# A retention head's keys: transposed by DMA in two planes of 16-bit halves, with the position factor on the values

## The chip, the cores and the metric

The kernel runs on one core of a Trainium2 chip. Its time is the device time of the whole program in microseconds, as the median of several runs. A core has a matrix engine (TensorE, PE in the profile), three engines for elementwise work (VectorE, DVE; ScalarE, ACT; GpSimd, POOL) and SyncE (SP), which here does nothing but issue DMAs, one after the other in one queue.

## The reference

One layer of a decoder in float32: 2048 tokens of width 1024, with 16 learned meta tokens ahead of them. The projection `w_in` gives eight groups of 512 columns. Four of them feed a gated short convolution, four a retention with 4 heads of width 128, computed in chunks of 128 tokens.

```python
hn = rms_norm(h, norm_g)                       # h: 16 meta tokens, then 2048 tokens
cx, cb, cc, cg, q, k, v, rg = split(hn @ w_in, 8)
conv_out = cb * causal_conv3(cc * cx) * silu(cg)
q, k = rotary(q, pos) * 128**-0.5, rotary(k, pos)        # 4 heads of width 128
# per head, with decay g per token, chunks n of 128 tokens, i and j positions in a chunk:
inner = ((q @ k.T) * g**(i - j) * (i >= j)) @ v
upd   = (k * g**(127 - j)).T @ v                         # sums over the chunk's tokens
state_next = g**128 * state + upd
cross = (q * g**(i + 1)) @ state
ret   = head_group_norm(inner + cross) * silu(rg)        # norm over the head's 128 columns
out   = rms_norm(h + concat(conv_out, ret) @ w_out, final_g)
```

The product `upd` sums over tokens, so it needs k and v with the tokens on the partitions. The projections come out of TensorE the other way, with the head's 128 columns on the partitions. Both k and v have to be transposed, chunk by chunk. The score product needs k untransposed.

## The kernel before

**Rounds and units.** The 2048 tokens are worked in two rounds of 1024, each as two halves `j` = 0 and 1 of 512 tokens (4 chunks). A round runs eight units: 0 to 3 are the heads, 4 to 7 the convolution groups. Round 0 takes them as 4, 0, 1, 2, 3, 5, 6, 7, round 1 as 0 to 7. The output projection with `w_out` follows.

**Quads.** A unit consists of two quads of projections; those of a head make K and V, and then Q and RG (the gate). A quad multiplies two blocks of weights by two of tokens with seven products instead of eight (Strassen's scheme in Winograd's form). A product is four steps in the contraction with three matmuls each (line L232), because every float32 operand is split in a high and a low part: low weight by high data, high by low, high by high. The products add up in PSUM banks named `pj`. Product 5 adds onto the bank that holds product 3, and ScalarE must have copied product 3 out before (`tc`, L239). The weights come by DMA (`ra`, L487, eight buffers), GpSimd forms their block sums, ScalarE casts the high part (`wh`, L110), VectorE subtracts for the low part (`wl`, L122); both lie in rings of three buffers, so the cast of one product's weights waits until TensorE has finished the product three before it.

**A head.** VectorE applies the rotary table to K and Q (L648 to L651). V goes through `part` and `cross`: ScalarE copies the float32 values apart into a plane of low and one of high 16-bit halves (`pl`, L667), SP issues a DMA that transposes each 128x128 block of both planes (`tr`, L660), and later `join` on ScalarE puts the halves together (`v`, L745) and multiplies each chunk by `rc2`, the squared row norms' factor (L748). After the second quad, for each half j: TensorE transposes the four chunks of K into PSUM (L768), ScalarE copies them out and multiplies by the position factor `kd_col`, which is g**-(j + 1) in column h (`kd`, L770), and TensorE makes four state updates (`up`, L777), which VectorE adds onto the decayed states (L780). Then follow the scores (L790), their mask on VectorE (`pm`, L792) with a factor `past_col` per row, the two products of the output (L800, L801) and the norm (L806 to L817). The normalised output is turned back during the next unit by the same means (`turn`: `apart`, L823, and `cross`; `finish`: L829 and L831).

**What sets the order.** The framework that builds the program schedules each engine's instructions by a model of time; hints of the form `issue_after` hold a step behind another instruction. The second quad calls a list of `steps`, one after each copied bank (after products 0, 2 and 3). For a head of the kernel before they are `split_late`, which takes V's half 0 apart, and the join of V's half 0; the join of half 1 follows the quad. Tiles named `kd`, `pm` and `t1` share a pool of two buffers (`brief`); `pl`, `tr`, `v`, `kv`, `qg` and others share a pool of sixteen (`gen`).

In round 0 each head also multiplies the meta tokens with its weights (L445) and makes its first state of them (L475).

Of the kernel before, what the change touches and what calls it, by code (L numbers as in the profile page):

```python
# [8 lines left out]
F32 = mybir.dt.float32  # L9
# [4 lines left out]
ALU = mybir.AluOpType  # L14

P = 128
# [4 lines left out]
NG = 4  # L21
EPS = 1e-6
HB = 512
NR = 2
# [23 lines left out]
def retention_constants():  # L48

    import numpy as np  # L50

    half = P // 2
    freqs = (1.0 / (10000.0 ** (np.arange(half) / half))).astype(np.float32)
    pos = np.arange(NMETA + SEQ, dtype=np.float32)
    ang = (freqs[:, None] * pos[None, :]).astype(np.float64)
    cos, sin = np.cos(ang), np.sin(ang)
    rot = np.stack([np.concatenate([cos, cos], 0), np.concatenate([sin, -sin], 0)], 1)

    lg = np.log(np.float32(1.0) - np.float32(2.0) ** (-5.0 - np.arange(NG, dtype=np.float32)))
    lg = lg.astype(np.float32).astype(np.float64)  # L60
    i = np.arange(P, dtype=np.float64)
    causal = (i[None, :] >= i[:, None]).astype(np.float64)
    past = np.stack([np.exp(-(P + i + 1) * g) for g in lg], 1)
    kd = np.stack([np.exp(-(i + 1) * g) for g in lg], 1)
    signed = np.concatenate([-sin[:, :NMETA], sin[:, :NMETA]], 0)
    rot_m = np.stack([np.concatenate([cos[:, :NMETA]] * 2, 0), signed], 0).transpose(2, 0, 1)
    rot_m = rot_m[:, :, None, :] * kd[P - NMETA :, None, :, None]
    row = np.stack([np.exp((P + i + 1) * g) * P**-0.5 for g in lg], 1)
    cols = np.concatenate([kd, EPS / (row * row), past], 1)
    chunk_decay = [float(np.exp(P * g)) for g in lg]  # L70
    return {
        "rot": rot.astype(np.float32),
        "rot_m": rot_m.reshape(NMETA, 2, NG, P).transpose(2, 0, 1, 3).astype(np.float32),
        "causal": causal.astype(np.float32),
        "cols": cols.astype(np.float32),
    }, chunk_decay
# [3 lines left out]
def hybrid_trunk(ctx: ExitStack, tc: tile.TileContext, t, out: bass.AP, chunk_decay):  # L80
# [4 lines left out]

    nc = tc.nc
    x = t["x"]

    const = ctx.enter_context(tc.tile_pool(name="const", bufs=1))
    small = ctx.enter_context(tc.tile_pool(name="small", bufs=2))  # L90
# [33 lines left out]
    def load_raw(loads):  # L124
        tiles = []
        for load in loads:
            a = raw()
            load(a)
            tiles.append(a)
        return tiles  # L130
# [213 lines left out]
    ones_r = const.tile([P, 1], F32R, name="ones_r")  # L344
    neg_half = const.tile([P, CH], F32, name="neg_half")
    meta_s = const.tile([P, KT, NMETA], F32, name="meta_s")
    cols = const.tile([P, 3 * NG], F32, name="cols")
    conv_w = const.tile([P, NG, 3], F32, name="conv_w")
    ret_g = const.tile([P, NG], F32, name="ret_g")
    causal = const.tile([P, P], F32, name="causal")  # L350
    conv_carry = [const.tile([P, 2], F32, name=f"carry{g}") for g in range(NG)]
    state = [const.tile([P, P], F32, name=f"state{h}") for h in range(NG)]
    kd_col, eps_col, past_col = (cols[:, NG * i : NG * (i + 1)] for i in range(3))

    def raw():
        return sb.tile([P, HB], F32, name="ra", tag="ra", bufs=RAW)
# [9 lines left out]
    def spread_factors(ss, rr, rr2, two_part):  # L366


        add(nc.vector, ss[:, 0, :], ss[:, 0, :], ss[:, 1, :])
        rc = small.tile([P, CH], F32, name="rc", tag="rc")  # L370
        v = rsqrt_mean(rc, ss[:, 0, :])
        spread(rc, P, rr, rr2, two_part)
        rc2 = small.tile([P, CH], F32, name="rc2", tag="rc2", bufs=2 * NR)
        nc.vector.tensor_tensor(out=rc2, in0=rc, in1=rc, op=ALU.mult)
        ev = small.tile([P, NG, CH], F32, name="ev", tag="ev", bufs=2 * NR)
        nc.vector.tensor_tensor(
            out=ev,
            in0=eps_col.rearrange("p (h c) -> p h c", c=1).broadcast_to([P, NG, CH]),
            in1=v.rearrange("p (h c) -> p h c", h=1).broadcast_to([P, NG, CH]),
            op=ALU.mult,  # L380
        )
        return rc2, ev

    def row_tile(name, pair):
        return sb.tile([P, BLK], F32, name=name, tag=f"rr{pair}", bufs=2)
# [298 lines left out]
    def head(h, r, m, rot_t, f, turning, blocks, ahead, sums, first=(), between=((), idle, idle)):  # L684
# [37 lines left out]
        def take(i, j, pp, c):  # L722
# [9 lines left out]
            else:  # L732
# [3 lines left out]
                nc.vector.tensor_tensor(out=d, in0=pp, in1=f[0][:, j * HB : (j + 1) * HB], op=ALU.mult)  # L736
                sg[j] = d

        def split_late():
            for j in late:  # L740
                v[j] = part(v[j])

        def join(j):
            a = gen("v")[:, :HB]
            nc.scalar.copy(out=halves(a), in_=planes(v[j]))  # L745
            for c in range(CH):
                cs = slice(c * P, (c + 1) * P)
                nc.scalar.mul(a[:, cs], a[:, cs], f[2][j][0][:, c : c + 1])  # L748
            v[j] = a

        quad(stationary(load_raw(w_loads(2 * h + 1))), m, take, (split_late, lambda: join(0)))
        catch_up(1)
        with tc.issue_after(copied[0].ins):
            join(1)
        between[2]()
        with tc.issue_after(queried[0].ins):
            next(sums, None)
# [5 lines left out]
        states = [state[h]]  # L763
        vt = []
        for j in range(2):
            tp = ps_misc()
            for c in range(CH):
                nc.tensor.transpose(tp[:, c * P : (c + 1) * P], k[j][:, c * P : (c + 1) * P], ident)  # L768
            kd = brief("kd")
            nc.scalar.mul(kd, tp, kd_col[:, h : h + 1])  # L770
            vj = v[j]
            vt.append(vj)
            last = r == NR - 1 and j == 1
            up = ps_misc()
            for c in range(CH - last):
                cs = slice(c * P, (c + 1) * P)
                nc.tensor.matmul(up[:, cs], kd[:, cs], vj[:, cs], start=True, stop=True)  # L777
            for c in range(CH - last):
                nxt = sb.tile([P, P], F32, name="state", tag="state", bufs=2 * CH)
                nc.vector.scalar_tensor_tensor(  # L780
                    out=nxt, in0=states[-1], scalar=chunk_decay[h], in1=up[:, c * P : (c + 1) * P],
                    op0=ALU.mult, op1=ALU.add,
                )
                states.append(nxt)

        for j in range(2):
            sc = ps_misc()
            for c in range(CH):
                cs = slice(c * P, (c + 1) * P)
                nc.tensor.matmul(sc[:, cs], k[j][:, cs], q[j][:, cs], start=True, stop=True)  # L790
            pm = brief("pm")
            nc.vector.scalar_tensor_tensor(  # L792
                out=pm.rearrange("p (c i) -> p c i", c=CH), in0=sc.rearrange("p (c i) -> p c i", c=CH),
                scalar=past_col[:, h : h + 1],
                in1=causal.rearrange("p (c i) -> p c i", c=1).broadcast_to([P, CH, P]), op0=ALU.mult, op1=ALU.mult,
            )
            o = ps_misc()
            for c in range(CH):
                cs = slice(c * P, (c + 1) * P)
                nc.tensor.matmul(o[:, cs], pm[:, cs], vt[j][:, cs], start=True, stop=False)  # L800
                nc.tensor.matmul(o[:, cs], q[j][:, cs], states[j * CH + c], start=False, stop=True)  # L801

            st = small.tile([P, CH, 6], F32, name="st", tag="st")
            mv = small.tile([P, CH, 2], F32, name="mv", tag="mv")
            for c in range(CH):
                nc.vector.bn_stats(out=st[:, c, :], in_=o[:, c * P : (c + 1) * P])  # L806
            for c in range(CH):
                nc.vector.bn_aggr(out=mv[:, c, :], in_=st[:, c, :])
            rs = small.tile([P, CH, 1], F32, name="rs", tag="rs")
            ev = f[2][j][1]  # L810
            add(nc.vector, rs, mv[:, :, 1:2], ev[:, h, :].rearrange("p (c a) -> p c a", a=1))
            rp = small.tile([P, CH, 1], F32, name="rp", tag="rp")
            nc.gpsimd.tensor_tensor(out=rp, in0=rs, in1=neg_half.rearrange("p (c a) -> p c a", a=1), op=ALU.pow)  # L813
            y = pm
            for c in range(CH):
                cs = slice(c * P, (c + 1) * P)
                nc.vector.tensor_scalar(  # L817
                    out=y[:, cs], in0=o[:, cs], scalar1=mv[:, c, 0:1], scalar2=rp[:, c, :],
                    op0=ALU.subtract, op1=ALU.mult,
                )  # L820

            def turn(j=j, y=y, apart=turning[0][:, j * HB : (j + 1) * HB], across=turning[1][:, j * HB : (j + 1) * HB]):
                nc.scalar.copy(out=planes(apart), in_=halves(y))  # L823
                cross(across, apart)

                nc.scalar.activation(sg[j], sg[j], AF.Silu)

                def finish():
                    nc.scalar.copy(out=halves(apart), in_=planes(across))  # L829
                    nc.vector.scalar_tensor_tensor(  # L830
                        out=sg[j], in0=apart, scalar=ret_g[:, h : h + 1], in1=sg[j], op0=ALU.mult, op1=ALU.mult  # L831
                    )
                    store_mixed(r, j, KH + h, sg[j])

                waiting[1].append(finish)

            waiting[0].append(turn)
# [249 lines left out]
```

## Time and profile before

| what | value |
|---|---|
| median of 3 runs (lowest to highest) | 876.3 us (876.18 to 877.04) |
| span of the profiled execution, first to last instruction | 874.9 us |
| PE busy | 863.1 us (99%), clock 0.997 on average |
| PE weight loads (beside the matmuls) | 711.8 us (81%) |
| DVE busy | 717.1 us (82%) |
| ACT busy | 474.8 us (54%) |
| POOL busy | 391.2 us (45%) |
| DMA | 143 GB/s on average |

The runs' times are those of executions without a profile; the profiled execution has its span only, and 874.9 stands 1.4 us below the median, which takes in what lies around the span. A matmul's end in the profile is modelled, so matmuls that follow each other overlap in the rows, and the step from start to start (12 matmuls of a product in 2.73 us) says more than a duration.

### The profile page before, as it was taken

The page shows a single profiled execution, that of the slowest core. Times are in us where ns is not written, and L with a number is a line of the kernel's source. Part 1 is how long each engine was busy: PE and PEld are TensorE (multiplying, and loading weights), DVE is VectorE, ACT ScalarE, POOL GpSimd, SP SyncE. Part 2 cuts the span into 40 slices and gives each one's busy share as a digit, 9 for nine tenths or more (in the row PEclk, how much of TensorE's full clock was granted, in tenths as well). Part 3 has the DMA queues.
Part 4 walks back from the last instruction along what each step waited for, and adds up shares of the span by engine and source line. Part 5 has one row for each costly group of instructions (what it writes and reads, how often), then busy time and mean ns, then how long its engine had stood idle before and what let it go on. Part 6 is the DMA issues. An engine that isn't in the chain of part 4 may idle for free.

```text
span 874.9 us, 12767 instructions
## 1 busy us (share of the span) xinstructions
PE 863.1 (99%) x4280; PEld 711.8 (81%) x4280; DVE 717.1 (82%) x1190; ACT 474.8 (54%) x883; POOL 391.2 (45%) x286
## 2 busy tenths in 40 slices
PE   8999999999999999999999999999999999999996
PEld 5878788878888778888888888888888888788885
DVE  6889898989887887989889898988767799656664
ACT  8675547374644654846464646444333465545553
POOL 0662332333235555352232333354646545678763
PEclk9999999999999999999999999999999999999998
DMA  9723235353556633854243444646222594455432
GB/s 336 220 81 81 63 75 143 109 145 97 129 185 181 190 112 97 292 166 121 61 120 133 108 158 86 214 100 211 64 73 67 172 339 132 162 159 188 154 129 76
DMA packets 110321, 125.32 MB, mean 143 GB/s; under 512 B 41456, under 2 KB 58672, under 8 KB 110256
## 3 DMA queue, kind: packets, MB, share of 16 engines
q1 hardware_dynamic: 109680, 124.11, 46.9%
q8 instruction: 34, 0.56, 0.3%
q10 hardware_dynamic: 576, 0.40, 0.1%
q14 instruction: 31, 0.25, 0.1%
HBM read 90.92 MB, written 25.17 MB: 133 GB/s over the span
## 4 chain that ended last, share of the span: by engine, by line
PE 91%; DVE 5%; issue 1%; ACT 1%; DMA 1%; POOL 0%; ACTq 0%; POOLq 0%; DVEq 0%
PE pj L232 72%; PE pj L289 10%; PE ms L800 2%; PE ms L801 2%; PE ms L790 2%; PE ms L777 1%; PE ms L445 1%; DVE wl L122 1%; PE ms L768 1%; DMA ra<-in_w_in 1%; DVE ml L122 1%; DVE c L523 0%; DVE ml L114 0%; DVE rot L648 0%; DVE yo L870 0%
## 5 line engine op out<-in xcount | busy, mean ns | idle before, releaser
L232 PE MATMUL pj<-mh,wl 128*128 128x512 f32 x1008 | 397.8, 395 | 1.5 <-ACT tc L239 1.2
L232 PE MATMUL pj<-mh,wh 128*128 128x512 f32 x1008 | 393.2, 390 | 0.0
L232 PE MATMUL pj<-ml,wh 128*128 128x512 f32 x1008 | 392.5, 389 | 0.0
L110 ACT CAST wh<-ra 128x512 fp32r<-128x512 f32 x216 | 133.9, 620 | 272.5 <-PE pj L232 226.0
L122 DVE TENSOR_TENSOR wl<-ra,wh 128x512 fp32r<-128x512 f32 x216 | 188.6, 874 | 45.6 <-ACT wh L110 45.1
L232 PEld LDWEIGHTS pj<-mh,wl 128*128 128x128 f32 x1008 | 189.3, 188 | 42.7 <-issue 2.7
L232 PEld LDWEIGHTS pj<-mh,wh 128*128 128x128 f32 x1008 | 189.2, 188 | 40.1
L232 PEld LDWEIGHTS pj<-ml,wh 128*128 128x128 f32 x1008 | 189.4, 188 | 37.8
L119 POOL TENSOR_TENSOR sa<-ra 128x512 f32<-128x512 f32 x36 | 53.0, 1473 | 99.7 <-DMA ra<-in_w_in 50.9
L122 POOL TENSOR_TENSOR ra<-sa,ra 128x512 f32<-128x512 f32 x36 | 51.8, 1438 | 80.2 <-DVE wl L122 79.0
L122 POOL TENSOR_TENSOR ra<-ra 128x512 f32<-128x512 f32 x36 | 58.0, 1611 | 59.4 <-PE ms L445 47.5
L149 POOL TENSOR_TENSOR ra<-ra 128x512 f32<-128x512 f32 x36 | 61.0, 1694 | 39.5 <-issue 26.7
L239 ACT COPY tc<-pj 128x512 f32<-128x512 f32 x108 | 62.6, 580 | 0.0
L289 PE MATMUL pj<-mh,mh 128*128 128x512 f32 x128 | 51.0, 400 | 1.8 <-ACT mh L967 1.1
L289 PE MATMUL pj<-mh,ml 128*128 128x512 f32 x128 | 50.0, 390 | 0.2 <-DVE ml L122 0.2
L289 PE MATMUL pj<-ml,mh 128*128 128x512 f32 x128 | 48.1, 392 | 0.0
L813 POOL TENSOR_TENSOR rp<-rs,neg_half 128x4 f32<-128x4 f32 x16 | 17.8, 1112 | 54.8 <-DVE rs L119 54.7
L870 DVE TENSOR_TENSOR yo<-pj,yo 128x512 f32<-128x512 f32 (+1 forms) x33 | 22.0, 673 | 22.6 <-PE pj L232 15.0
L585 POOL TENSOR_TENSOR c<-c,rr 128x512 f32<-128x512 f32 x14 | 26.4, 1884 | 29.8 <-DVE c L626 18.1
L110 ACT CAST wh<-sa 128x512 fp32r<-128x512 f32 x36 | 22.2, 617 | 22.9 <-PE pj L232 22.9
L876 POOL TENSOR_TENSOR z<-yo,final_g 128x512 f32<-128x512 f32 x16 | 26.0, 1627 | 18.9 <-DVE yo L870 18.9
L817 DVE TENSOR_SCALAR pm<-ms,mv,rp 128x128 f32<-128x128 f32 x64 | 21.9, 404 | 12.4 <-POOL rp L813 12.3
(152 smaller groups left out, 1209.2 us busy)
## 6 DMA issues: line engine op xcount, KB each, us to landing
ra<-in_w_in SPq DMA_DIRECT2D x126, 256.0 KB, 2.8
x<-in_xT SPq DMA_DIRECT2D x48, 256.0 KB, 4.8
w<-in_w_out SPq DMA_DIRECT2D x32, 256.0 KB, 5.0
ra<-mixed SPq DMA_DIRECT2D x32, 256.0 KB, 2.9
yo<-in_x SPq DMA_DIRECT2D x32, 256.0 KB, 4.5
ra<-in_x SPq DMA_DIRECT2D x16, 256.0 KB, 3.6
mixed<-c SPq DMA_DIRECT2D x16, 256.0 KB, 2.4
mixed<-qg SPq DMA_DIRECT2D x16, 256.0 KB, 2.5
```

Of the source, the lines that this page charges most:

```text
L110: nc.scalar.copy(out=hi, in_=src)
L119: eng.tensor_tensor(out=out, in0=a, in1=b, op=ALU.add)
L122: eng.tensor_tensor(out=out, in0=a, in1=b, op=ALU.subtract)
L149: summed[0] = nc.gpsimd.tensor_tensor(out=a12, in0=a12, in1=a11, op=ALU.subtract)
L232: nc.tensor.matmul(bank, a[:, ks], b, start=first and kt == 0 and n == 0, stop=kt == KH - 1 and n == 2, skip_group_check=not first,)
L239: copied[0] = nc.scalar.copy(out=c, in_=bank)
L289: nc.tensor.matmul(banks[i], a[:, ks], b, start=half + kt + n == 0, stop=half == 1 and kt == KH - 1 and n == 2,)
L585: eng.tensor_tensor(out=out, in0=a, in1=b, op=ALU.mult)
L813: nc.gpsimd.tensor_tensor(out=rp, in0=rs, in1=neg_half.rearrange("p (c a) -> p c a", a=1), op=ALU.pow)
L817: nc.vector.tensor_scalar(out=y[:, cs], in0=o[:, cs], scalar1=mv[:, c, 0:1], scalar2=rp[:, c, :], op0=ALU.subtract, op1=ALU.mult,)
L870: last[0] = nc.vector.tensor_tensor(out=y[:, cs], in0=pp[:, cs], in1=y[:, cs], op=ALU.add)
L876: nc.gpsimd.tensor_tensor(out=ys[i][j], in0=y, in1=final_g[:, j * HB : (j + 1) * HB], op=ALU.mult)
```

## The change

The four transposes of K on TensorE (L768) and the copy out of PSUM with the factor (L770) go. Instead each half of K takes V's way, by `split_keys` and `join_keys`. `split_keys(0)` runs in the second quad's first step, `split_keys(1)` in the second step behind V's join of half 0, `join_keys(0)` in a third step, and `join_keys(1)` after V's join of half 1. The joined K is a plain copy. The position factor `kd_col` moves to the values: `spread_factors` makes `vk` = `kd_col` x `rc2` per head and chunk, and V's join multiplies by it. The output product of the scores uses the same V, so the mask's factor per row, `past_col`, becomes one number per head, g**-128, since g**-(128 + i + 1) is that times the g**-(i + 1) that V now has.

```diff
-    past = np.stack([np.exp(-(P + i + 1) * g) for g in lg], 1)
-    chunk_decay = [float(np.exp(P * g)) for g in lg]
+    chunk_decay = [float(np.exp(P * g)) for g in lg], [float(np.exp(-P * g)) for g in lg]
...
-        rc2 = small.tile([P, CH], F32, name="rc2", tag="rc2", bufs=2 * NR)
+        rc2 = small.tile([P, CH], F32, name="rc2", tag="rc2")
         nc.vector.tensor_tensor(out=rc2, in0=rc, in1=rc, op=ALU.mult)
+        vk = small.tile([P, NG, CH], F32, name="vk", tag="vk", bufs=2 * NR)
+        nc.vector.tensor_tensor(
+            out=vk,
+            in0=kd_col.rearrange("p (h c) -> p h c", c=1).broadcast_to([P, NG, CH]),
+            in1=rc2.rearrange("p (h c) -> p h c", h=1).broadcast_to([P, NG, CH]),
+            op=ALU.mult,
+        )
...
+        across_k, kt = [None, None], [None, None]
+
+        def split_keys(j):
+            across_k[j] = part(k[j])
+
+        def join_keys(j):
+            kt[j] = brief("kd")
+            nc.scalar.copy(out=halves(kt[j]), in_=planes(across_k[j]))
+
         def split_late():
             for j in late:
                 v[j] = part(v[j])
+            split_keys(0)
 
         def join(j):
             a = gen("v")[:, :HB]
             nc.scalar.copy(out=halves(a), in_=planes(v[j]))
             for c in range(CH):
                 cs = slice(c * P, (c + 1) * P)
-                nc.scalar.mul(a[:, cs], a[:, cs], f[2][j][0][:, c : c + 1])
+                nc.scalar.mul(a[:, cs], a[:, cs], f[2][j][0][:, h, c : c + 1])
             v[j] = a
 
-        quad(stationary(load_raw(w_loads(2 * h + 1))), m, take, (split_late, lambda: join(0)))
+        def middle():
+            join(0)
+            split_keys(1)
+
+        quad(stationary(load_raw(w_loads(2 * h + 1))), m, take, (split_late, middle, lambda: join_keys(0)))
         catch_up(1)
         with tc.issue_after(copied[0].ins):
             join(1)
+            join_keys(1)
...
-            tp = ps_misc()
-            for c in range(CH):
-                nc.tensor.transpose(tp[:, c * P : (c + 1) * P], k[j][:, c * P : (c + 1) * P], ident)
-            kd = brief("kd")
-            nc.scalar.mul(kd, tp, kd_col[:, h : h + 1])
-            vj = v[j]
+            kd, vj = kt[j], v[j]
...
-                scalar=past_col[:, h : h + 1],
+                scalar=past[h],
```

The schedule moves with it. TensorE in head 2 of round 1, at the border of products 4 and 5 of the second quad (the second operand of an L232 names the data tile `mh` or `ml`; `wh` and `wl` are the weights' parts), before:

```order
L232 MATMUL pj<-mh_4141,wh 128x512
L777 MATMUL ms<-v,kd 128x128
L768 MATMUL ms<-ident,kv 128x128 x4
L777 MATMUL ms<-v,kd 128x128 x3
L232 MATMUL pj<-mh_3880,wl 128x512
```

The same border now, with the two matmuls on either side:

```order
L232 MATMUL pj<-mh_4141,wl 128x512
L232 MATMUL pj<-ml_4142,wh 128x512
L232 MATMUL pj<-mh_4141,wh 128x512
L232 MATMUL pj<-mh_3880,wl 128x512
L232 MATMUL pj<-ml_3881,wh 128x512
L232 MATMUL pj<-mh_3880,wh 128x512
```

Products 4 and 5 follow each other directly now; the state updates have moved behind product 6 of this quad.

ScalarE around products 2 and 3 of the same quad, before:

```order
L667 COPY pl_5091<-kv_4992 128x1024
L823 COPY apart_3975<-pm_4854 128x1024
L110 CAST wh_5064<-ra_5039 128x512
L770 ACTIVATE kd_5239<-ms_5234,cols_75 128x512
L110 CAST wh_5068<-ra_5037 128x512
L239 COPY tc_5127<-pj_5076 128x512
L745 COPY v_5129<-tr_5026 128x2x512
L748 ACTIVATE v_5129<-v_5129,rc2_3333 128x128 x4
L110 CAST wh_5072<-ra_5041 128x512
L239 COPY tc_5148<-pj_5135 128x512
```

And now (`pl_5091` is made of K's half 0, `pl_5135` of its half 1):

```order
L674 COPY pl_5087<-kv_4988 128x1024
L840 COPY apart_3975<-pm_4850 128x1024
L674 COPY pl_5091<-kv_4940 128x1024
L110 CAST wh_5060<-ra_5035 128x512
L110 CAST wh_5064<-ra_5033 128x512
L239 COPY tc_5127<-pj_5072 128x512
L762 COPY v_5129<-tr_5022 128x2x512
L674 COPY pl_5135<-kv_5002 128x1024
L765 ACTIVATE v_5129<-v_5129,vk_3331 128x128 x4
L110 CAST wh_5068<-ra_5037 128x512
L239 COPY tc_5152<-pj_5139 128x512
```

The first split of K stands ahead of two casts of weights, the second between the two parts of V's join, and both stand ahead of the last `tc`, the copy of product 3. L770 is gone.

SP's queue in the same head, before (`ra` are loads of weights):

```order
L660 DMA_TRANSPOSE across_3976<-apart_3975 128x8x128
L660 DMA_TRANSPOSE tr_5026<-pl_5025 128x8x128
L487 DMA ra_5232<-in_w_in 128x512
L660 DMA_TRANSPOSE tr_5092<-pl_5091 128x8x128
L660 DMA_TRANSPOSE across_3976<-apart_3975 128x8x128
L487 DMA ra_5491<-in_w_in 128x512
L487 DMA ra_5493<-in_w_in 128x512
L487 DMA ra_5495<-in_w_in 128x512
```

And now, from the transpose of V's half 1:

```order
L667 DMA_TRANSPOSE tr_5088<-pl_5087 128x8x128
L667 DMA_TRANSPOSE across_3976<-apart_3975 128x8x128
L667 DMA_TRANSPOSE tr_5092<-pl_5091 128x8x128
L494 DMA ra_5485<-in_w_in 128x512
L494 DMA ra_5487<-in_w_in 128x512
L667 DMA_TRANSPOSE tr_5136<-pl_5135 128x8x128
L494 DMA ra_5489<-in_w_in 128x512
L502 DMA mixed2_91<-qg_4748 128x4x128
```

The transposes of K's halves have come in ahead of and between the loads of the next quad's weights.

More of the change, by code (lines that the diff above doesn't have):

```diff
@@ L68, in retention_constants @@
     row = np.stack([np.exp((P + i + 1) * g) * P**-0.5 for g in lg], 1)
-    cols = np.concatenate([kd, EPS / (row * row), past], 1)
-    chunk_decay = [float(np.exp(P * g)) for g in lg]
+    cols = np.concatenate([kd, EPS / (row * row)], 1)
+    chunk_decay = [float(np.exp(P * g)) for g in lg], [float(np.exp(-P * g)) for g in lg]
     return {
@@ L87, in hybrid_trunk @@
     x = t["x"]
+    chunk_decay, past = chunk_decay
     const = ctx.enter_context(tc.tile_pool(name="const", bufs=1))
@@ L346, in hybrid_trunk @@
     meta_s = const.tile([P, KT, NMETA], F32, name="meta_s")
-    cols = const.tile([P, 3 * NG], F32, name="cols")
+    cols = const.tile([P, 2 * NG], F32, name="cols")
     conv_w = const.tile([P, NG, 3], F32, name="conv_w")
@@ L352, in hybrid_trunk @@
     state = [const.tile([P, P], F32, name=f"state{h}") for h in range(NG)]
-    kd_col, eps_col, past_col = (cols[:, NG * i : NG * (i + 1)] for i in range(3))
+    kd_col, eps_col = (cols[:, NG * i : NG * (i + 1)] for i in range(2))
     def raw():
@@ L381, in spread_factors @@
         )
-        return rc2, ev
+        return vk, ev
     def row_tile(name, pair):
```

## The prediction

> **What bounds the kernel now.** I read the busy times first, then the chain that ended last, then who waits for whom, then the start times of single instructions.
>
> ```profile
> PE 863.1 (99%) x4280; PEld 711.8 (81%) x4280; DVE 717.1 (82%) x1190; ACT 474.8 (54%) x883; POOL 391.2 (45%) x286
> PE 91%; DVE 5%; issue 1%; ACT 1%; DMA 1%; POOL 0%; ACTq 0%; POOLq 0%; DVEq 0%
> ```
>
> TensorE is busy for 99% of the span and holds 91% of the chain. A modelled matmul end can hide a stall, so I looked for TensorE's own waits and for the two kinds of head.
>
> ```profile
> PE pj L232 <- ACT tc L239: 1.2, 1, 1.2
> ACT wh L110 <- PE pj L232: 248.9, 151, 5.1
> 195.00:243.00 48.00, 48.00 (x275) 40.06 (x274) 43.26 (x86) 26.37 (x46) 14.90 (x12) 1.00 0.46 121
> 496.00:542.00 46.00, 46.00 (x239) 39.22 (x239) 41.69 (x80) 24.78 (x41) 14.46 (x10) 1.00 0.46 126
> ```
>
> The windows' columns are length, then PE, PEld, DVE, ACT, POOL busy, granted clock, DMA share, GB/s; one window is a head of round 0, the other of round 1. In all heads TensorE is full at clock 1.00, VectorE has about 4 us to spare per head, ScalarE 21. ScalarE mostly waits for TensorE to free a weight buffer. TensorE waited once for ScalarE, 1.2 us for a product's copy (tc, L239); keep that row in mind. So a slot taken from TensorE is time, as long as no other queue then comes last.
>
> **What is removed.** 64 transposes, 16 groups of four (j = 0 and 1 of 8 heads).
>
> ```profile
> L768 PE MATMUL ms<-ident,kv 128*128 128x128 f32 x64 | 9.6, 272 | 0.0
> 96.90 0.40 PE L232 MATMUL pj<-mh,wh 128*128 128x512 f32 x1
> 97.14 0.60 PE L768 MATMUL ms<-ident,kv 128*128 128x128 f32 x4
> 97.49 0.48 PE L232 MATMUL pj<-mh,wl 128*128 128x512 f32 x1
> 97.81 0.40 PE L232 MATMUL pj<-ml,wh 128*128 128x512 f32 x1
> ...
> 194.16 0.44 PE ms L768 x4
> ```
>
> From the start at 96.90 to that at 97.81 are 0.91 us, of which two ordinary steps of 0.2275 (12 matmuls take 2.73) are not the transposes': a group costs 0.455 us. 16 x 0.455 = 7.3; a piece of the chain gives 16 x 0.44 = 7.0. I take 7.2 us. The mean of 272 ns is a duration that overlaps its neighbours. [...]
>
> **What is added, off the path first.** ScalarE: 16 splits and 16 joins of 128x1024 halves, less 16 copies out of PSUM (L770).
>
> ```profile
> L770 ACT ACTIVATE kd<-ms,cols 128x512 f32<-128x512 f32 x16 | 11.0, 689 | 3.9 <-PE ms L768 3.8
> L745 ACT COPY v<-tr 128x1024 uint16<-128x1024 uint16 x16 | 21.8, 1360 | 0.0
> L667 ACT COPY pl<-kv 128x1024 uint16<-128x1024 uint16 x7 | 7.3, 1046 | 0.0
> tr<-pl SPq DMA_TRANSPOSE x16, 3.1
> 490.61 1.24 SPq L660 DMA_TRANSPOSE tr<-pl  x1
> 495.82 3.98 SPq L487 DMA_DIRECT2D ra<-in_w_in  x3
> ```
>
> 16 x (1.05 + 1.36 - 0.69) = 27.5 us more, ScalarE 474.8 to 502: still far from the span, so only its order matters. SP: 16 transposes of 1.24 us, 20 us of issue. K1's stands behind two loads of weights that wait for buffers (the row at 495.82); they go ahead once w5's low part is made, before K1's split is done, so neither delays the other by more than about 1 us. VectorE: four small multiplications (vk), under 1 us, before the heads; taking the factor as a constant instead of a column is costed at nothing. The path of a key is now 1.05 + 3.1 + 1.36 = 5.5 us, against 0.44 + 0.69. I cost it at nothing, by the head-2 rows below: K0's split can begin once the copy named apart is done, at 490.87 + 1.05 = 491.9, so the key is there by 497.4; the state matmuls (UP, L777, now L794) come after product 6, whose end is 494.24 + 4 x 2.73 = 505.2. That leaves 7.8 us. K1's split follows the join of v (495.52 + 1.37 = 496.9), its key is there by 502.4, and its UP comes another 24 matmuls (5.4 us) after the first, at 510.6: 8.2 us.
>
> **What is moved, and costs.** The scheduler fills the place of the transposes with projections, as the order shown with the change has it for head 2 of round 1: products 4 and 5 of the second quad now follow each other on TensorE without a gap. Product 5 adds onto the bank that holds product 3, and must wait until ScalarE has copied that (the last tc). On ScalarE, K1's split now stands between the join of v and that copy. The same stretch in the trace of before:
>
> ```profile
> 490.87 1.05 ACT L823 COPY apart<-pm 128x1024 uint16<-128x1024 uint16 x1 [0.29 <-DVE pm L817]
> 448.20 0.39 PE L232 MATMUL pj<-mh,wl 128*128 128x512 f32 x1
> 448.48 0.62 ACT L110 CAST wh<-ra 128x512 fp32r<-128x512 f32 x1 [1.91 <-PE pj L232]
> 540.31 0.39 PE L232 MATMUL pj<-mh,wl 128*128 128x512 f32 x1
> 540.59 0.62 ACT L110 CAST wh<-ra 128x512 fp32r<-128x512 f32 x1 [1.52 <-POOL ra L122]
> 494.24 0.39 PE L232 MATMUL pj<-mh,wl 128*128 128x512 f32 x1
> 494.52 0.62 ACT L110 CAST wh<-ra 128x512 fp32r<-128x512 f32 x1 [1.49 <-POOL ra L122]
> 495.52 1.37 ACT L745 COPY v<-tr 128x1024 uint16<-128x1024 uint16 x1
> 498.62 0.58 ACT L239 COPY tc<-pj 128x512 f32<-128x512 f32 x1
> 499.68 0.38 PE L777 MATMUL ms<-v,kd 128*128 128x128 f32 x2
> 500.93 0.48 PE L232 MATMUL pj<-mh,wl 128*128 128x512 f32 x1
> ```
>
> 494.24 is the start of product 3. w5's cast begins 0.28 later because product 2 gives back its buffer then: the row names POOL, but the other heads of the round, whatever their row names, have the same 0.28 (448.20 and 448.48, 540.31 and 540.59), so a ScalarE that is ready sooner starts no sooner.
>
> The copy ends at 498.62 + 0.58 = 499.20, 4.96 after product 3's start; product 4's last slot ends at 499.68, 5.44 after it, and product 5 starts at 500.93. So the copy had 1.73 us, of which the UP and TR block gave 1.25. Now the copy ends at 4.96 + 0.95 (a split next to other work) = 5.91, and product 5 could start at 5.44: it waits about 0.5 us. Bounds: 0, if the copy is on time, and 1.21, the one such wait in the trace:
>
> ```profile
> 744.39 0.57 ACT L239 COPY tc<-pj 128x512 f32<-128x512 f32 x1
> 745.01 0.50 PE L232 MATMUL pj<-mh,wl 128*128 128x512 f32 x1 [1.21 <-ACT tc L239]
> 186.65 0.48 PE L475 MATMUL ms<-mk 16*128 16x128 f32 x2
> 187.84 0.50 PE L232 MATMUL pj<-mh,wl 128*128 128x512 f32 x1
> ```
>
> I take 0.5, since all its terms are rows of that very place. Where it applies: heads 1, 2, 3 of round 1 (head 0 there has no finish step and multiplies v after the copy). In round 0 products of the meta tokens (186.65 to 187.84, 1.19 us) stand between products 4 and 5; heads 0 and 2 keep them and are covered, in heads 1 and 3 the order now puts them behind product 5. Five places, 2.5 us. The next cover to go would be that of w0 of the next quad, whose cast now stands behind the K0 join (1.36) as well. Between nothing, since ScalarE has 21 us idle in a head, and 1.36 in one head, I take 0.2 for all of them, nearer to nothing.
>
> **Sum.** -7.2 + 2.5 + 0.2 = -4.5 us. The span goes from 874.9 to 870.4; the median of the runs, 876.3, lies 1.4 above that span, so 871.8.
>
> **Rivals.** (B) The copies come in time, as when the removed L770 and idle time of 1.49 ahead of w5 let ScalarE start earlier: against it, that idle is a wait for TensorE's buffer, which comes no earlier. Time 876.3 - 7.2 = 869.1. (C) The wait is larger: w5's cast itself is late. K0's split (0.95) stands between apart (490.87, waiting for VectorE) and w5, in place of L770 (0.6) and 0.77 us of the rest; if VectorE normalises pm 0.8 us later than now, every further 0.1 us is one on TensorE in five heads. With 1.21 each, 6.1 us: 875.2 to 877. For it: in round 1 the last projection of the quad ahead now stands behind the O block, so VectorE's order shifts. (D) Slower: the keys come late to UP, for 5.5 us against 1.1. It decides where a head's transposed key lands more than 8 us late; to be slower than 878.05 each of the 8 heads must lose (7.2 + 1.75) / 8 = 1.1 us beyond that cover. A transpose held on SP behind three waits like that at 495.82 (3 x 3.98 = 11.9, so 3.7 beyond the cover) in the four heads of round 1 gives 876.3 - 7.2 + 4 x 3.7 = 883.9. Against it: one such wait stands ahead of K1, not three, and a transpose lands 3.1 us after its issue in the median of 16. [...]
>
> **Chances.** Forecast (870.4 to 873.4) 0.50; B 0.25, with a trifle below it; C 0.18, of which 0.08 is still faster by over 0.2%; D 0.07. About 0.2% (1.75 us) is what a measurement tells from no change here. Faster 0.83, same 0.10, slower 0.07. The range goes from B, 868.7, to C's price by the 1.21 row, 875.2.
>
> **What would show it.** Right: no L768; L232's first matmul of product 5 waiting for ACT tc L239, about 0.5 us, five times, and not in heads 0 and 2 of round 0; ScalarE near 502 us; span near 870.4. B: no such waits, span near 867.7. C: these waits near 1 us, with w5's cast late behind apart. D: L794 waiting for ACT kd. Wrong altogether would be new gaps in the convolution units (270 to 371 us), where the chain runs over VectorE and which I take as shifted only.

## The result, and the profile after

The changed kernel takes 873.66 us in the median (871.39 to 875.31, 7 runs) against 876.35: a ratio of 0.9961, with a 95% interval of 0.9949 to 0.9972. On two other chips it was 871.63 and 871.81 (5 runs each, 0.9939 with 0.9926 to 0.9951, and 0.9938 with 0.9925 to 0.9950). It is faster by some 2.7 to 5.6 us; 871.8 was forecast. The profiled execution took 872.54 with a span of 870.7. Of the kernels below, one (the turn left out of the kernel before) had two executions of 1074 and 1445 us, the latter at a granted clock of 0.557, and its figures are those of the other ten.

The busy line and the chain of the changed kernel's page:

```profile
PE 856.9 (98%) x4216; PEld 704.6 (81%) x4216; DVE 707.0 (81%) x1194; ACT 498.5 (57%) x899; POOL 395.0 (45%) x286
PE 82%; DVE 5%; ACT 4%; issue 2%; DMA 2%; SPq 0%; POOLq 0%; POOL 0%; ACTq 0%; DVEq 0%
```

From its list of who waits for whom, two of TensorE's rows (total, times, longest):

```profile
PE pj L232 <- ACT tc L239: 2.5, 6, 1.7
PE pj L289 <- DVE ml L122: 1.0, 1, 1.0
```

64 matmuls are gone. ScalarE is at 498.5 us (502 was forecast), and it now holds 4% of the chain. TensorE waits for the copy `tc` six times instead of once. Where, the timeline of TensorE says (start, duration, and in brackets the wait and its releaser):

```profile
137.88 0.50 PE L232 MATMUL pj<-mh,wl 128*128 128x512 f32 x1 [0.17 <-ACT tc L239]
233.13 0.50 PE L232 MATMUL pj<-mh,wl 128*128 128x512 f32 x1 [0.16 <-ACT tc L239]
450.28 0.50 PE L232 MATMUL pj<-mh,wl 128*128 128x512 f32 x1 [0.17 <-ACT tc L239]
495.87 0.50 PE L232 MATMUL pj<-mh,wl 128*128 128x512 f32 x1 [0.17 <-ACT tc L239]
541.43 0.50 PE L232 MATMUL pj<-mh,wl 128*128 128x512 f32 x1 [0.17 <-ACT tc L239]
740.81 0.50 PE L232 MATMUL pj<-mh,wl 128*128 128x512 f32 x1 [1.66 <-ACT tc L239]
```

The first five are product 5 of the second quad in heads 1 and 3 of round 0 and heads 1, 2, 3 of round 1, the five places that were named. The sixth is in the output stage, where it was 1.21 before. A bracket understates what is lost, because the end of the matmul ahead is modelled: at the fourth place two starts ahead of it and one behind it are

```profile
490.10 0.39 PE L232 MATMUL pj<-mh,wl 128*128 128x512 f32 x1
...
495.32 0.39 PE L232 MATMUL pj<-mh,wh 128*128 128x512 f32 x1
...
496.21 0.40 PE L232 MATMUL pj<-ml,wh 128*128 128x512 f32 x1
```

(product 3's first, product 4's last, and product 5's second). The step from 495.32 to 495.87 is 0.55 instead of 0.2275, and the one from there to 496.21 is 0.34, so 0.32 and 0.11, together 0.44 us, are lost. It is the same within 0.02 at all five places. ScalarE in the same stretch:

```profile
490.38 0.62 ACT L110 CAST wh<-ra 128x512 fp32r<-128x512 f32 x1 [0.57 <-PE pj L232]
490.91 0.58 ACT L239 COPY tc<-pj 128x512 f32<-128x512 f32 x1
491.39 1.36 ACT L762 COPY v<-tr 128x1024 uint16<-128x1024 uint16 x1
492.60 1.04 ACT L674 COPY pl<-kv 128x1024 uint16<-128x1024 uint16 x1
493.55 1.28 ACT L765 ACTIVATE v<-v,vk 128x128 f32<-128x128 f32 x4
494.73 0.61 ACT L110 CAST wh<-ra 128x512 fp32r<-128x512 f32 x1
495.24 0.58 ACT L239 COPY tc<-pj 128x512 f32<-128x512 f32 x1
```

The cast for product 5 begins 0.28 after product 3's start (490.10), as it did before, and from there ScalarE has no idle time until the copy. From the join (491.39) to the multiplication (493.55) are 2.16 us; before, they were 496.92 - 495.52 = 1.40. So K's split costs 0.76 here, not the 0.95 from its start to the next instruction's: it begins 1.21 after the join's start, and before, the multiplication began 1.40 after it, at the end of a join of 1.37. Those 0.19 us are no loss.

Where the time went, by stages between starts of matmuls (L232, the first of a quad) in the two timelines:

| stage | before | after | difference |
|---|---|---|---|
| start to the first quad of head 0, round 0 | 57.05 | 57.11 | +0.06 |
| heads of round 0 | 212.65 | 210.28 | -2.37 |
| convolution units of round 0 | 82.00 | 81.28 | -0.72 |
| begin of round 1, first quad of its head 0 | 41.81 | 42.58 | +0.77 |
| heads of round 1 | 184.21 | 181.81 | -2.40 |
| convolution units of round 1, begin of the output | 155.04 | 155.06 | +0.02 |
| rest of the output | 142.14 | 142.58 | +0.44 |

The sum is -4.2, the difference of the spans. The heads give 4.77 us. What the transposes took there can be read by starts. Eight of the 16 groups stand alone between two projections, like the one of the prediction, 0.45 us each. The other eight stand beside other small matmuls, for example behind eight matmuls of a state update. Such a place in the timeline of before:

```profile
103.07 1.05 PE L777 MATMUL ms<-v,kd 128*128 128x128 f32 x8
103.96 0.60 PE L768 MATMUL ms<-ident,kv 128*128 128x128 f32 x4
104.31 0.48 PE L232 MATMUL pj<-mh,wl 128*128 128x512 f32 x1
```

and one of the changed kernel:

```profile
501.45 1.05 PE L794 MATMUL ms<-v,kd 128*128 128x128 f32 x8
502.25 0.48 PE L232 MATMUL pj<-mh,wl 128*128 128x512 f32 x1
```

From the first update to the projection were 1.24 us with the four transposes, and are 0.80 without: 0.44 a group. All 16 are 7.1 us; the five waits of 0.44 give back 2.2. That leaves 4.9, near the 4.77 of the table.

### The profile page after: what moved, and what is told of

Its sections match the earlier page's. It is cut to its first block, busy times and chain, and to the rows that moved or that the text cites. A ratio compares the mean times of both kernels' runs of the same rounds, so it can differ in the third digit from the quotient of the medians.

```text
span 870.7 us, 12707 instructions
## 1 busy us (share of the span) xinstructions
PE 856.9 (98%) x4216; PEld 704.6 (81%) x4216; DVE 707.0 (81%) x1194; ACT 498.5 (57%) x899; POOL 395.0 (45%) x286
## 4 chain that ended last, share of the span: by engine, by line
PE 82%; DVE 5%; ACT 4%; issue 2%; DMA 2%; SPq 0%; POOLq 0%; POOL 0%; ACTq 0%; DVEq 0%
PE pj L232 71%; PE pj L289 3%; DVE ml L122 2%; PE ms L818 2%; PE ms L807 2%; PE ms L817 2%; PE ms L794 2%; DMA t<-sums_w 1%; PE ms L452 1%; ACT wh L110 1%; DVE wl L122 1%; ACT v L762 1%; ACT v L765 1%; ACT tc L239 1%; DMA x<-in_xT 1%
## 5 line engine op out<-in xcount | busy, mean ns | idle before, releaser
L232 PE MATMUL pj<-mh,wl 128*128 128x512 f32 x1008 | 397.0, 394 | 2.6 <-ACT tc L239 2.5
L232 PE MATMUL pj<-mh,wh 128*128 128x512 f32 x1008 | 393.0, 390 | 0.0
L232 PE MATMUL pj<-ml,wh 128*128 128x512 f32 x1008 | 392.8, 390 | 0.0
L232 PEld LDWEIGHTS pj<-mh,wl 128*128 128x128 f32 x1008 | 189.3, 188 | 46.3 <-ACT tc L239 5.5
L232 PEld LDWEIGHTS pj<-mh,wh 128*128 128x128 f32 x1008 | 189.2, 188 | 39.6
L232 PEld LDWEIGHTS pj<-ml,wh 128*128 128x128 f32 x1008 | 189.4, 188 | 37.7
L149 POOL TENSOR_TENSOR ra<-ra 128x512 f32<-128x512 f32 x36 | 60.2, 1672 | 48.4 <-issue 38.5
L122 POOL TENSOR_TENSOR ra<-ra 128x512 f32<-128x512 f32 x36 | 56.9, 1580 | 50.2 <-PE ms L452 27.9
L289 PE MATMUL pj<-mh,mh 128*128 128x512 f32 x128 | 50.7, 397 | 1.2 <-ACT mh L113 0.7
L289 PE MATMUL pj<-mh,ml 128*128 128x512 f32 x128 | 50.0, 390 | 1.0 <-DVE ml L122 1.0
L289 PE MATMUL pj<-ml,mh 128*128 128x512 f32 x128 | 48.0, 392 | 0.0
L887 DVE TENSOR_TENSOR yo<-pj,yo 128x512 f32<-128x512 f32 (+1 forms) x33 | 22.1, 674 | 31.8 <-PE pj L232 23.4
L119 POOL TENSOR_TENSOR yo<-yo,tc 128x512 f32<-128x512 f32 x18 | 28.6, 1589 | 8.8 <-ACT tc L239 8.8
```

The costliest lines, as they stand in the source:

```text
L119: eng.tensor_tensor(out=out, in0=a, in1=b, op=ALU.add)
L122: eng.tensor_tensor(out=out, in0=a, in1=b, op=ALU.subtract)
L149: summed[0] = nc.gpsimd.tensor_tensor(out=a12, in0=a12, in1=a11, op=ALU.subtract)
L232: nc.tensor.matmul(bank, a[:, ks], b, start=first and kt == 0 and n == 0, stop=kt == KH - 1 and n == 2, skip_group_check=not first,)
L289: nc.tensor.matmul(banks[i], a[:, ks], b, start=half + kt + n == 0, stop=half == 1 and kt == KH - 1 and n == 2,)
L887: last[0] = nc.vector.tensor_tensor(out=y[:, cs], in0=pp[:, cs], in1=y[:, cs], op=ALU.add)
```

## The experiments

**The changed kernel again, for its spread.**

> The changed kernel once more, for a second trace and its spread. My account: five waits of product 5 for the copy of product 3, 0.3 us each, in the same five heads, and a time of 871 to 875. Rival (the DMAs of the keys disturb other transfers, in some runs more than in others): the runs spread over 3 us or more, and the trace shows the difference at the begin of a round, where the chain runs over loads, not in the heads.

871.63 us (870.92 to 872.47), and the trace has the same five waits of 0.16 and 0.17. The spread of 3.9 us on the first chip did not return, so nothing here shows that the keys' DMAs cause it. No trace of a run of this kernel above 873 exists, and what made those runs longer stays open. Three of the four have a mean granted clock of 0.996, as the trace with a stretch of low clock in the last section has; that is a hint and no more.

**K's second split behind the copy.**

```diff
         def middle():
             join(0)
-            split_keys(1)
+        def third():
+            split_keys(1)
+            join_keys(0)
...
-        quad(..., (split_late, middle, lambda: join_keys(0)))
+        quad(..., (split_late, middle, third))
```

> The split of K's half 1 moved behind the copy of product 3. My account (the split stands ahead of that copy): the five waits go, 5 x 0.32 = 1.6 us less than the changed kernel. Rival (the copy is late for another reason, the casts of weights): the waits stay, no change within 0.3 us. Rival (the key then comes late): L797 or its neighbours, the state updates, wait for kd.

874.47 us (873.55 to 875.99), ratio 0.9974 (0.9963 to 0.9984): 2.8 us slower than the changed kernel beside it. My expectation was wrong, though the waits did go. The first of TensorE's waits:

```profile
PE pj L232 <- DVE wl L122: 2.2, 3, 0.8
```

The place in the timeline, head 2 of round 1:

```profile
500.86 1.05 PE L797 MATMUL ms<-v,kd 128*128 128x128 f32 x8
502.65 0.47 PE L232 MATMUL pj<-mh,wl 128*128 128x512 f32 x1 [0.73 <-DVE wl L122]
```

The wait for `tc` is left only in the output stage. In its place the next quad's first product waits for the low part of its weights, in heads 1, 2, 3 of round 1, 0.7 to 0.8 each by the brackets and 1.0 by the starts. The heads of round 1 take 183.59 us instead of 181.83 in the trace of the changed kernel beside it.

ScalarE's queue runs without a pause from the cast for product 5 to that for the next quad, so one could take its length for the cause. But the cast of these weights' high part is not late: it begins at 499.39, and at 499.38 in the changed kernel (the quad ahead at 481.82 and 481.94). What differs is VectorE's queue:

```profile
500.39 0.69 DVE L655 TENSOR_TENSOR rot<-qg,rot_t 64x512 f32<-64x512 f32 x1
501.09 0.69 DVE L656 TENSOR_TENSOR rot<-qg,rot_t 64x512 f32<-64x512 f32 x1
501.81 1.29 DVE L122 TENSOR_TENSOR wl<-ra,wh 128x512 fp32r<-128x512 f32 x2
```

In the changed kernel the subtraction stands ahead of these two steps of Q's rotation, the first of which begins at 501.52:

```profile
500.81 0.68 DVE L122 TENSOR_TENSOR wl<-ra,wh 128x512 fp32r<-128x512 f32 x1
```

It is so in all three heads. So the edit moved a step on ScalarE, and the order that the scheduler then gave VectorE made the wait. Most of the rest of the loss in this trace is a stretch of low clock (0.84 and 0.82 in two windows of 5 us, some 1.6 us; last section).

**No turn of the keys.**

```diff
-            across_k[j] = part(k[j])
+            kt[j] = k[j]
...
-            kt[j] = brief("kd")
-            nc.scalar.copy(out=halves(kt[j]), in_=planes(across_k[j]))
+            pass
```

> Leaves out the turning of the keys altogether: the state updates take the keys as they are, with no split, DMA or join, and no TensorE transposes. My account: 7.2 us less than before less what the new order costs elsewhere (about 1 us at the begin of round 1), 869 to 870, so 1.6 us or a little more below the changed kernel, with no product-5 waits. Rival (the transposes on TensorE were worth only some 3 to 4 us): the same as the changed kernel, about 873. Rival (the keys' DMAs make the spread): its runs agree within 1.2 us, as those of the kernel before do.

875.27 us (874.52 to 877.74), ratio 0.9984 (0.9975 to 0.9992). With less work on TensorE, ScalarE and SP than the changed kernel has, it is 3.6 us slower. Every expectation missed, mine by 5 us, and without any DMA of a key its runs still spread over 3.2 us. The first of TensorE's waits:

```profile
PE ms L816 <- DVE pm L808: 3.1, 3, 1.4
```

The output product waits for VectorE's mask, which stands behind two steps of K's rotation (head 1 of round 0: rotation from 157.39, mask at 158.81). In the changed kernel it stands ahead of them (154.43, rotation from 157.72). Leaving the work out changed the schedule, so this kernel is no measure of what the work costs.

**The factor alone.** From the changed kernel: keys transposed by TensorE again and copied plainly, with no split and join of keys; the factor stays on the values.

```diff
-            split_keys(0)
...
-            split_keys(1)
...
-            join_keys(1)
...
-            kd, vj = kt[j], v[j]
+            tp = ps_misc()
+            for c in range(CH):
+                nc.tensor.transpose(tp[:, c * P : (c + 1) * P], k[j][:, c * P : (c + 1) * P], ident)
+            kd = brief("kd")
+            nc.scalar.copy(out=kd, in_=tp)
```

> Only the factor is moved: keys are transposed by TensorE as before and copied plainly, the values carry the position factor. My account: the same as before within 0.5 us (876.3). Rival (the factor's place matters, by VectorE's small multiplications or another order): off by over 1 us.

876.77 us against 876.77, ratio 0.9998 (0.9989 to 1.0007). The factor's place is worth nothing that these runs can tell. Its trace settles one row of the table above: the begin of round 1 has the longer wait (L289 for VectorE's `ml`, 1.0 us) here too, with TensorE's transposes in place. Before had 0.2 there, the changed kernel 1.0, and two traces of one and the same kernel (early splits, late join, below) 1.0 and 0.4. So nothing ties the +0.77 to the change.

**The price of a transpose: twice as many.**

```diff
+                for _ in range(2):
-                nc.tensor.transpose(tp[:, c * P : (c + 1) * P], ...)
+                    nc.tensor.transpose(tp[:, c * P : (c + 1) * P], ...)
```

> The kernel before with every TensorE transpose of a key issued twice. If a group of four costs 0.455 us wherever it stands, as I priced it: 16 x 0.455 = 7.3 us more, 884. If what counts is the step from start to start of a 128-wide matmul inside a block (0.09 us) and the border to the next projection is paid anyway: 64 x 0.09 = 5.8 us more, 882.4. If TensorE has slack there: under 2 us more.

883.5 us (882.02 to 885.31) against 876.88, ratio 1.0077 (1.0065 to 1.0089): 6.6 us more, by the interval 5.7 to 7.8. In the trace the heads are longer by 2.82 in round 0 and 3.29 in round 1, 6.1 us; the doubled kernel lacks two small stalls of round 0, 0.4 us by the starts, that the trace of before has. A row of eight beside the row of four that the prediction used (97.14, next start 97.49):

```profile
96.50 1.04 PE L769 MATMUL ms<-ident,kv 128*128 128x128 f32 x8
97.29 0.48 PE L232 MATMUL pj<-mh,wl 128*128 128x512 f32 x1
```

From the block's start to the projection's are 0.79 us with eight transposes and 0.35 with four, so four more cost 0.44 here, and the step behind is 0.32 with either. TensorE's slots are on the path. A group is worth 0.36 to 0.49 us by the runs and 0.44 by the rows, which the first account (0.455) fits; the runs do not tell it from the second (0.36).

**Both splits early.**

```diff
-            split_keys(0)
+            for j in range(2):
+                split_keys(j)
...
         def middle():
             join(0)
-            split_keys(1)
```

> Both splits of K in the second quad's first step, so that the split of half 1 stands ahead of the cast for product 5. The join of K's half 1 then stands ahead of the cast of the next quad's first weights. Account A (ScalarE is the bound from product 3 to the next quad's first weights, in heads 1 to 3 of round 1): no wait of product 5, but the next quad's first product waits 0.7 to 1 us for its low part wl in those three heads; time as with the late split, some 2 us above the changed kernel. Account B (only the copy of product 3 matters): 1.6 us below the changed kernel, 870.

872.77 us (871.98 to 874.05), ratio 0.9956 (0.9945 to 0.9968): between the two accounts in time. Product 5 no longer waits, and the next quad's first product waits 0.8 in heads 1, 2, 3 of round 1, as account A has it (a fourth such wait, of 0.79, stands in round 0 at 128.26). The join of K's half 1 now comes ahead of the next quad's first cast (head 2 of round 1):

```profile
496.90 1.35 ACT L753 COPY kd<-tr 128x1024 uint16<-128x1024 uint16 x1
498.11 1.13 ACT L110 CAST wh<-ra 128x512 fp32r<-128x512 f32 x2
...
500.90 0.46 PE L232 MATMUL pj<-mh,wl 128*128 128x512 f32 x1 [0.80 <-DVE wl L122]
```

But VectorE's two steps of Q's rotation (498.65 and 499.35) stand ahead of the subtraction (500.06) here too. The later cast and this order both delay it, and this run does not separate them.

**Both splits early, the second join late.** Besides the edit above:

```diff
             join(1)
+        with tc.issue_after(joined[0].ins):    # the last multiplication of join(1)
             join_keys(1)
```

> Both splits of K early, and the join of K's half 1 held behind V's join of half 1, so that neither the copy of product 3 nor the cast of the next quad's first weights stands behind one of them more than before. Account A: both waits go, 1.6 us or a little more below the changed kernel, 870. Account B: as with the early split alone. If the later key is late for the state updates: L794's successor waits for kd, in every head, 0.5 us or more.

870.79 us (870.35 to 871.28), ratio 0.9931 (0.9919 to 0.9943).

> Both splits early, K's second join late, again, on the same chip as the changed kernel. Account A: 1 us less than the changed kernel (1.6 us of waits gone, some of it taken by waits of the output product for VectorE's mask in round 1). If the difference seen between two calls was one of chips: the same as the changed kernel within 0.3 us.

Beside the changed kernel on one chip it took 870.36 us, ratio 0.9922 (0.9908 to 0.9935), and the changed kernel

> The changed kernel again, beside the next two on one chip. 871 to 874, about 0.994 to 0.996 of the kernel before.

871.81. So 1.45 us are gained by the edit, which moves two steps in ScalarE's queue; the two intervals overlap, but no run of the one lies among those of the other (870.09 to 871.11, and 871.27 to 872.51). The brackets leave TensorE one kind of wait in the heads:

```profile
PE ms L818 <- DVE pm L810: 0.4, 2, 0.2
```

ScalarE at the end of the same quad, and then TensorE at the state update of K's half 1:

```profile
496.73 1.13 ACT L110 CAST wh<-ra 128x512 fp32r<-128x512 f32 x2
...
503.93 1.34 ACT L753 COPY kd<-tr 128x1024 uint16<-128x1024 uint16 x1
505.32 0.94 PE L795 MATMUL ms<-v,kd 128*128 128x128 f32 x6
```

VectorE's subtraction (498.17) stands ahead of the rotation (499.68) again. Both waits are gone, as account A has it. But the key joined at 505.27 is late: the state update of half 1 starts at 505.32, 0.37 after the matmul ahead of it instead of 0.23, and no bracket shows it. In heads 1, 2, 3 of round 1 that costs 0.2 us each by the starts.

The stages say where the gain lies, against the changed kernel's trace on the same chip. The heads of round 1 take 181.97 us against 181.80: what the three waits give (1.3) is taken by the late keys (0.7) and by the output product waiting for VectorE's mask (0.8 by the starts, at 421.28 and 467.02). The heads of round 0 take 207.80 against 210.29. Two waits are 0.9 of that; with the rest goes another order of TensorE's small matmuls, which stand between the projections in 17 blocks instead of 23, and it was not separated. The convolution units of round 0 give back 0.8. So this version beats both kernels, but that ScalarE's queue between product 3 and the next quad was the limit is not shown.

**The turn left out of the kernel before.**

```diff
-            tp = ps_misc()
-            for c in range(CH):
-                nc.tensor.transpose(tp[:, c * P : (c + 1) * P], k[j][:, c * P : (c + 1) * P], ident)
             kd = brief("kd")
-            nc.scalar.mul(kd, tp, kd_col[:, h : h + 1])
+            nc.scalar.mul(kd, k[j], kd_col[:, h : h + 1])
```

> The kernel before without the transposes of the keys: ScalarE multiplies the untransposed key by the factor, at the same place, and nothing turns it. Leaves out the turn. It shows what TensorE's slots alone are worth. By 0.455 a group: 7.2 us less than before, 869.3. By 0.09 a transpose: 5.8 us less, 870.7. If other engines take the place at once, as without any turn in the changed kernel (waits of the output product for VectorE's mask): 1 to 3 us less.

876.2 us (875.53 to 877.55) against 876.88, ratio 0.9993 (0.9985 to 1.0002): nothing that is clear of noise, where 7.1 us of slots are gone. The first two expectations missed, and the gain is below the 1 to 3 us of the third. It was run once more for a trace:

> The kernel before without the keys' turn, for a trace (its runs showed no gain: 876.4 against 876.9). If VectorE's mask and norm come too late once TensorE is faster: L797, the output product, waits for pm in each head of round 0 or 1, and these waits add up to about the 5.8 us of slots that are gone. If it is the weights' casts: L232 waits for wl or tc instead. Leaves out the turn.

876.24 us. TensorE's waits:

```profile
PE ms L797 <- DVE pm L789: 3.7, 5, 1.5
PE pj L232 <- ACT tc L239: 2.9, 3, 1.3
```

VectorE, and then TensorE, at one of the two longest, in head 1 of round 0:

```profile
159.26 0.69 DVE L648 TENSOR_TENSOR rot<-kv,rot_t 64x512 f32<-64x512 f32 x1
159.96 0.68 DVE L649 TENSOR_TENSOR rot<-kv,rot_t 64x512 f32<-64x512 f32 x1
160.68 0.75 DVE L789 SCALAR_TENSOR_TENSOR pm<-ms,cols,causal 128x512 f32<-128x512 f32 x1
161.48 0.49 PE L797 MATMUL ms<-v,pm 128*128 128x128 f32 x2 [1.51 <-DVE pm L789]
```

The mask stands behind two steps of K's rotation in VectorE's queue. In the changed kernel it stands ahead of them, and with both splits early and the late join too (154.08, rotation from 154.79); TensorE does not wait in that head there. Of the expectation, mask and copies both came: 3.7 us, and 1.6 in two new waits for `tc`. By the starts the heads lose 7.6 us more than before in late matmuls, about what the slots gave, and take 397.09 us against 396.85. So the slots' 7.1 us were not gained here, since the order that went with the edit made TensorE wait for other queues; in the changed kernel's order the heads gained 4.77.

**GpSimd in place of VectorE for one addition of the output stage.** The version with the late join, and

```diff
-                add(nc.vector if pair == 1 else nc.gpsimd, y, y, c)
+                add(nc.gpsimd, y, y, c)
```

> The same, and GpSimd in place of VectorE makes the output stage's additions of pair 1, where VectorE's first one lasts 1.78 us and TensorE then waits 1.2 to 1.8 us for the last tc. If that addition is what holds the copy: the wait goes, 1 to 1.7 us less than with the late join alone (869 to 870), and no run shows the stretch of halved clock that one trace had right behind that wait. If the squares' place in ScalarE's queue holds it whatever engine adds: the same time.

870.66 us (869.54 to 871.87), ratio 0.9924 (0.9910 to 0.9938): no difference to the version without it (870.36). The wait did shrink, from 1.74 to 0.46 (then for `wl`), but the stage gained only 0.55 us, and its trace lost 0.53 at the program's start and 0.64 at the begin of round 1 (868.9 us of span against 868.3). What this edit is worth is below what these runs tell apart.

## Why the prediction was right

- **The mechanism.** The order was read rightly. The copy of product 3 became late in the five places that were named and in no other head, because K's second split stands ahead of it, while the cast for product 5 did not move (rival C is out, its cast is 0.28 after product 3's start). No copy came in time there (B is out). No state update waits for a key (D is out): their group in the changed kernel (busy time and mean, then idle time before) shows no idle time, by the starts no update that follows a projection is late either, and a transpose lands 3.2 us after issue as the median of 32.

```profile
L794 PE MATMUL ms<-v,kd 128*128 128x128 f32 x120 | 16.1, 276 | 0.0
```

- **The slots, -7.2.** Sized well: 7.1 by the starts, and doubling them cost 6.6 (5.7 to 7.8). That one group between two projections was taken for all 16 did little harm, since a group beside other small matmuls costs 0.44. The row of durations, 272 ns, would have been off by a factor of 2.5: by the starts a transpose took 0.11.
- **The five waits, +2.5.** 5 x 0.44 = 2.2. The step ahead was shorter than thought: the copy ended 5.72 after product 3's start and not 5.91, since the split cost 0.76 and not 0.95. The longer step behind the wait, 0.11, was not counted.
- **The next quad's weights, +0.2.** Not seen in the changed kernel. With the split moved, a wait of 0.7 to 0.8 does stand at that place, but where the split is late it is VectorE's subtraction that comes late and not the cast that the prediction named.
- **The rest, taken as nothing:** +0.06 - 0.72 + 0.77 + 0.02 + 0.44 = +0.57. Of the -0.72, 0.6 is a wait for the weights' low part in the trace of before (291.12, 0.32 by its bracket) that no trace of the changed kernel has. The +0.77 is the wait at the begin of round 1. The +0.44 is the wait for `tc` in the output, 1.66 instead of 1.21; it was 1.33 and 1.62 in two other traces of the changed kernel. VectorE's four multiplications for `vk`, put at under 1 us, take 2.9: 0.15 and 0.17 for round 0 (43.07, 53.18), 1.27 each for round 1 (304.25, 345.07).
- **From span to time.** 1.4 us were added, the median less one execution's span; the profiled execution has 872.54 - 870.7 = 1.8.

The heads came out at -4.77 for -4.5, the rest at +0.57 for nothing. These offset each other, and that the span, 870.7, lies within 0.3 of the 870.4 is luck in part. The median of the first chip, 873.66, is 1.9 above the forecast: within the range to 875.2, but just outside the band of 870.4 to 873.4 that had the chance of 0.50. The two other chips' medians lie within 0.2 of the forecast, though their differences from the kernel before, 5.1 and 5.6, are above its 4.5. What sets the first chip's runs apart is open.

With TensorE at 99% of the span before, the path of longer latency through ScalarE and SP (5.5 us a key by the prediction's rows, against 1.1) gave the shorter time here, 873.66 against 876.35.

## What to carry to other kernels

When work is taken from the fullest engine, ask which queue of another engine then comes last. An edit of one queue can change the order that the scheduler gives the others: here, when a step was moved on ScalarE, VectorE's rotation came ahead of the weights that TensorE needed, and one wait was only exchanged for another. So compare the order of every queue ahead of a new wait, and the time of each stage, before you name a cause. An experiment that leaves work out lets the scheduler make another order, and its time is not the price of that work: here the kernel with less work was slower by 3.6 us, while doubling the same work cost 6.6, near the 7.1 that the starts give. Price small matmuls and waits by starts, from the last large matmul ahead to the second one behind: brackets of 0.17 were 0.44 by the starts, and late keys of 0.2 had none.

## What the runs showed of the hardware

**A stretch of low clock behind a short stall.** In the trace of the kernel with the late split, TensorE waits 1.77 us in the output stage; the starts are then 0.43 us apart instead of 0.2275, and the granted clock (the column behind POOL's busy time) is 0.84 and 0.82 in two windows of 5 us:

```profile
740.00:745.00 5.00, 3.23 (x12) 2.34 (x11) 4.16 (x6) 2.72 (x6) 2.26 (x2) 0.84 0.36 108
745.00:750.00 5.00, 5.00 (x20) 4.05 (x19) 1.89 (x3) 1.85 (x4) 2.72 (x2) 0.82 0.74 260
```

TensorE's timeline there, some rows of it:

```profile
742.07 0.50 PE L232 MATMUL pj<-mh,wl 128*128 128x512 f32 x1 [1.77 <-ACT tc L239]
743.71 0.63 PE L232 MATMUL pj<-mh,wl 128*128 128x512 f32 x1
744.14 0.63 PE L232 MATMUL pj<-ml,wh 128*128 128x512 f32 x1
746.70 0.44 PE L232 MATMUL pj<-ml,wh 128*128 128x512 f32 x1
```

It lasts 3.4 us (743.4 to 746.8) and costs about 1.6. The same wait of 1.66 in the changed kernel and of 1.74 in the version with the late join has no such stretch: the granted clock is 1.00 there in each window of 5 us from 735 to 750. What decides whether the stretch comes, no run here shows.

**An addition of 1.78 us beside GpSimd.** In the changed kernel the addition on VectorE ahead of the wait of 1.66 takes 1.78 us with GpSimd at work beside it, and one of the same form 0.68 where GpSimd is not at work (no row of GpSimd from 740.98 to 744.63):

```profile
736.38 1.78 DVE L119 TENSOR_TENSOR yo<-yo,tc 128x512 f32<-128x512 f32 x1
741.46 0.68 DVE L119 TENSOR_TENSOR yo<-yo,tc 128x512 f32<-128x512 f32 x1
735.88 1.73 POOL L119 TENSOR_TENSOR sa<-ra 128x512 f32<-128x512 f32 x1 [0.94 <-DVE wl L122]
```

It ends 0.55 us after GpSimd's (737.61), when GpSimd is at the next one (from 737.69, 1.62). Why it lasts that long is not shown: VectorE's L887 at 738.26, of the same shape, takes 0.69 beside that next one.
